# The weight lane of the feed-forward layers moves three steps at each turn in place of one

## The chip, the cores and the metric

The kernel runs on one core of a Trainium2 chip. The core has five instruction queues that work side by side: TensorE (PE, matrix products; PEld is its loading of weights), VectorE (DVE), ScalarE (ACT), GpSimd (POOL) and SyncE (SP, which here only issues DMA transfers). The metric is the device time of one execution in microseconds (us), the median over runs.

## The reference

One inference step of a two-layer decoder trunk, for a prompt of 1024 tokens with 16 meta tokens ahead of it, and for 8 running sequences with one new token each: 1048 columns in all, 1024 features. Layer 0 mixes with an SSD block (Mamba-2), layer 1 with a gated linear recurrence (RG-LRU). After each mixer stands the part that this case is about, a feed-forward layer of 4096 hidden features with a squared ReLU, between two RMS norms:

```python
def sq_relu_mlp(x, w1, w2):
    h = jax.nn.relu(x @ w1)
    return (h * h) @ w2

h = rms_norm(x, p["norm_ffn_pre"][i])
x = x + rms_norm(sq_relu_mlp(h, p["ffn_w1"][i], p["ffn_w2"][i]), p["norm_ffn_post"][i])
```

Everything is float32. The outputs are the new activations and the new states of both mixers.

## The kernel before

**Numbers in two halves.** A float32 operand is scaled by a power of two and split into two float16 tiles, a rounded half and the rest. A product then takes three float16 matmuls (half by half, half by rest, rest by half). The activations `U` (input of a feed-forward layer) and `H` (its hidden features) are kept like that, and so are the weights.

**Columns and strips.** The 1048 columns are worked in three pieces of 350, 350 and 348 (`c`). A weight matrix comes in strips of 256 output columns and 1024 input rows, 1 MB each. In a feed-forward layer the 4096 hidden features are worked in four blocks `b` of 1024. Each block takes four strips of `w1` (kind h in block 0, kind H after it), which produce `H`, and then four strips of `w2`, which add to the result `acc` (kind S in blocks 0 to 2, kind 2 in block 3).

**Units.** In blocks 1 to 3 the `w1` strips, and in blocks 0 to 2 the `w2` strips, go through `unit` (L1363): one strip with one column piece. It splits the product into two by two quadrants and works with seven smaller products in place of eight (Strassen's scheme; `product`, L380). It needs sums of weight quadrants (`wp`) beside the strip itself (`wh`), and sums of activations (`TT` from `U`, `HT` from `H`). The first product of a unit uses `wp`, the second `wh` with `TT` or `HT`. A unit of kind H has 84 matmuls, one of kind S about 90. It takes four of the eight PSUM banks (`mm`), so that two units can be on their way; ACT copies one product out (`z<-mm`), DVE adds the others into a tile `z`. For `w1`, ACT and DVE then form the squared ReLU and split it into `H`, and in the first two strips of a block `t_sums` (L1332) makes `HT`, its sums on POOL.

**The lane of the weights.** `wlane` (L406) is a Python generator that emits the instructions for one strip after the other. For each strip it emits, with a `yield` between the pieces:

1. the load of the 1 MB into one of two `ws` buffers (`load_strip`, L259; it is emitted while the strip ahead of it is converted);
2. the largest magnitude of each row, on DVE (`rm`, or `r` and `r4s` for kinds S and 2);
3. the scale (`strip_scale`, L264): a small matmul on PE spreads the rows' maxima (`mm<-ident,rm`), DVE takes the largest (`wgb`) and some ten tiny operations make the scale `s`, `sq`;
4. here the lane stops as long as more strips are ready than `ahead` allows. A strip with `wp` counts as two, and `ahead` is 3 within the blocks of units, 1 or 2 around them;
5. the sums (`sums`, L356): `wp` from ACT and DVE, three pairs of instructions, then four additions on POOL in place in `ws`;
6. the halves of the strip (`split`, L277): ACT writes the rounded half of `wh`, DVE the rest, in two instructions; for kinds S and 2 in four parts.

There are five `wh` buffers; a strip with `wp` takes two.

**Who moves the lane.** A main loop emits units and calls `tick` (L129) twice in each, once in its middle (in `unit`) and once at its end. `tick` moves each lane on by one `yield`: the lane of the weights, and others, such as the norm at a layer's border or the activation sums. A strip has three units and so six turns. When the main loop needs the next strip (`wneed`, L426) and it isn't ready, the lane is moved on until it is: whatever is left of a conversion is emitted there in one go. `first_phase` (L616) and `last_phase` (L567), at the start and the end of a layer, call `tick` as well.

**Order on the engines.** The order of emission is a priority. A planner in the framework lays the instructions of each engine out in time by its own cost estimates, and inserts all waits. On each engine it takes the instruction of highest priority among those whose inputs and buffers it expects to be there, so one of lower priority can move ahead into a gap. On the chip each engine then works through its list in order.

All instructions of this part are issued through one helper, so the profile has them all on L91 (earlier ones on L94): groups are told apart by tile names.

Of the kernel before, what the change touches and what calls it, by code (L numbers as in the profile page):

```python
# [60 lines left out]
class Carve:  # L61


    def __init__(self, tiles):
        self.free = [[t, 0] for t in tiles]
# [54 lines left out]
class Body:  # L120
    def __init__(self, ctx, tc, a):
        self.ctx, self.tc, self.nc, self.a = ctx, tc, Engines(tc), a
        self.lanes = []
        self.last_tab = None
        self.mmi = 0
        self.yfs = {}


    def tick(self):  # L129

        for lane in list(self.lanes):
            if next(lane, self) is self:
                self.lanes.remove(lane)

    def drain(self):
        while any(l is not self.wl for l in self.lanes):
# [1102 lines left out]
    def ffn(self, l):  # L1239
# [5 lines left out]
        HT = fp.tile([P, 3, NSUM, 3, 2, CW // 2], F16, name="HT")  # L1245
        U = self.U
        sctx = ExitStack()
        for b in range(4):
            H = fp.tile([P, 3, KT, 2, CW], F16, tag="H", name="H")
            rs = {}  # L1250

            def square(c, s, r):

                n = WC[c] // 2
                Hv = H[:, c, 2 * s:2 * s + 2, :, :2 * n].rearrange("p j s n -> p s j n")
                h = r.rearrange("p (j n) -> p j n", j=2)
                parts = [(0, n, 2 * n), (1, 0, 2 * n)] if self.summed(b, s) else [(slice(0, 2), 0, 2 * n)]
                nc.scalar.activation(Hv[:, 0], h, AF.Square)
                nc.scalar.activation(r, r, AF.Square)
                for j, o, e in parts:  # L1260
                    nc.vector.tensor_tensor(Hv[:, 1, j, o:e], h[:, j, o:e], Hv[:, 0, j, o:e], op=OP.subtract)
                if self.summed(b, s):
                    t = self.t_sums(r.rearrange("p (i n) -> p i n", i=4), Hv[:, :, 0, :n], HT[:, c, s, :, :, :n])
                    next(t)
                    self.lanes.append(t)

            def evac(s, w, m, c, ps):
                n = WC[c]
                if m == 0:
                    rs[s, c] = fp.tile([P, 2 * CW], F32, tag="r", name="r", bufs=RBUF)  # L1270
                r = rs[s, c]
                nc.scalar.activation(r[:, m * n:m * n + n], ps, AF.Relu, scale=w[2])
                if m:
                    square(c, s, rs.pop((s, c))[:, :2 * n])

            if b == 0:
                self.first_phase([self.wneed() for _ in range(3)], act, evac)
                sp = sctx.enter_context(tc.tile_pool(name=f"sum{l}", bufs=1, side="right", reuse_waits="tile"))
                TT = sp.tile([P, 3, 4, 3, 2, CW // 2], F16, name="TT")
                w = self.wneed()  # L1280
                for c in range(3):
                    for m in range(2):
                        ps = self.mm()
                        self.bundle(ps[:, :WC[c]], w[0], m, act, c)
                        evac(3, w, m, c, ps[:, :WC[c]])
                        self.tick()
                tl = self.input_sums(U, TT, fp)
                self.lanes.append(tl)
                self.ahead = 3
            else:  # L1290
                while tl in self.lanes:
                    self.tick()
                for s in range(4):
                    w, _, ti = self.wneed()
                    for c in range(3):
                        z = self.unit(w, self.parts(U, TT, c), c, 4, fp)
                        nc.scalar.activation(z, z, AF.Relu, scale=ti)
                        square(c, s, z)
                        self.tick()
            if b < 3:  # L1300
                for s in range(4):
                    w, inv, _ = self.wneed()
                    for c in range(3):
                        z = self.unit(w, self.parts(H, HT, c), c, NSUM, fp)
                        z = z.rearrange("p (m n) -> p m n", m=2)
                        o = acc[:, c, 2 * s:2 * s + 2, :WC[c]]
                        if b == 0:
                            nc.scalar.activation(o, z, AF.Copy, scale=inv)
                        else:
                            nc.vector.scalar_tensor_tensor(o, z, inv, o, op0=OP.mult, op1=OP.add)  # L1310
                        self.tick()
                if b == 2:
                    self.ahead = 2
            else:
                sctx.close()
                hact = self.act_of(H)
                self.open_bnd()

                def evac2(piece, mm, ps, inv, o):
                    c, lo, hi = piece  # L1320
                    nc.vector.scalar_tensor_tensor(o, ps, inv, acc[:, c, mm, lo:hi], op0=OP.mult, op1=OP.add)

                ws = [self.wneed()[:2] for _ in range(4)]
                if l == 0:
                    self.last_phase(ws, hact, 1, self.xd[0], self.xd[1], 2, evac2)
                else:
                    self.last_phase(ws, hact, 3, self.xd[2], [self.a["y01"][0], self.a["y01"][1], self.a["y2"]], None, evac2)
                    self.drain()
                    self.bndctx.close()
# [62 lines left out]


    def lru(self):
        nc, tc, ty = self.nc, self.tc, self.tiny
        a, v = self.a, self.v
        sctx = ExitStack()
# [154 lines left out]
        for s in range(4):  # L1552
            w, inv, _ = self.wneed()
# [118 lines left out]
```

## Time and profile before

| | |
|---|---|
| median of 3 runs | 2915.55 us (2909.4 to 2917.27) |
| the profiled execution | 2920.68 us |
| its span in the profile | 2918.8 us |
| mean granted TensorE clock | 0.954 |
| PE, DVE, ACT, POOL busy | 90%, 75%, 46%, 23% |
| DMA | 229 MB, 79 GB/s in the mean |

The span is the time from the first to the last instruction. "Granted clock" is the share of full speed that the chip gave TensorE. A table by stage cuts the span at given times and lists each engine's busy time within. A timeline row has the start, the length, the engine, the line, the operation with its output and inputs, and the count of instructions merged in it; brackets show how long the engine had been idle before, and what ended that. In a row of groups the busy time and the mean length of one in nanoseconds stand before the last bar, the idle time ahead of the group behind it.

### The profile page before, as it was taken

To read this page: it belongs to the slowest core of one execution; us is meant where nothing else is said; L and a number is where in the kernel's file an instruction comes from. 1 tells how busy PE (TensorE), PEld (TensorE's weight loads), DVE (VectorE), ACT (ScalarE), POOL (GpSimd) and SP (SyncE) were. 2 spreads that over 40 slices of the span, in tenths; PEclk is the share of its full clock that TensorE was granted. 3 is DMA by queue.
4 is the path that set the end of the run, shared out by engine and by line. 5 is a ranking of instruction groups with operands and counts; after the bars stand their busy time and mean duration, and the time that the engine had idled before them with its cause. 6 is when DMAs were issued, how large, how long until landed. Compare 5 with 4: busy or idle time off the path is not lost. (4 is left out here: it accounts for less than half of the span.)

```text
span 2918.8 us, 56796 instructions
## 1 busy us (share of the span) xinstructions
PE 2636.0 (90%) x23318; PEld 2089.8 (72%) x23318; DVE 2184.9 (75%) x5152; ACT 1329.8 (46%) x2148; POOL 668.5 (23%) x863
## 2 busy tenths in 40 slices
PE   5999999999999999889788899989999879889898
PEld 2666666666666668779788776665667879889776
DVE  6888977897745867778777689678785777777676
ACT  4544555545543453452442444577564343352342
POOL 3212212221110035421311100132024531221201
PEclk9999999999999999899898999999999989899899
DMA  3233233332345210111021133111220111111122
GB/s 139 77 105 109 86 100 110 108 108 94 113 159 222 100 58 30 45 44 45 30 88 59 45 107 112 65 42 56 94 101 16 45 44 45 45 32 57 36 80 92
DMA packets 52756, 229.14 MB, mean 79 GB/s; under 512 B 9056, under 2 KB 18416, under 8 KB 31632
## 3 DMA queue, kind: packets, MB, share of 16 engines
q1 hardware_dynamic: 46112, 190.81, 19.0%
q0 software_dynamic: 6384, 34.71, 3.0%
q8 instruction: 182, 2.98, 0.4%
q14 instruction: 78, 0.64, 0.1%
HBM read 186.28 MB, written 39.22 MB: 77 GB/s over the span
## 5 line engine op out<-in xcount | busy, mean ns | idle before, releaser
L91 PEld LDWEIGHTS <-wh 128*128 128x128 f16 x17040 | 1534.1, 100 | 639.5 <-ACT wh L91 104.5
L91 PE MATMUL mm<-U,wh 128*128 128x350 f16 (+3 forms) x7056 | 1015.2, 301 | 12.2 <-ACT rr L91 11.6
L91 PE MATMUL mm<-H,wh 128*128 128x175 f16 (+5 forms) x5664 | 569.4, 255 | 8.9 <-DVE wh L91 8.8
L91 POOL TENSOR_TENSOR ws<-ws 128x256 f32<-128x256 f32 (+1 forms) x192 | 214.1, 1115 | 656.5 <-DVE wp L91 602.9
L91 DVE TENSOR_TENSOR z<-z,mm 128x175 f32<-128x175 f32 (+3 forms) x648 | 232.8, 372 | 97.8 <-ACT z L91 71.2
L91 PEld LDWEIGHTS <-wp 128*128 128x128 f16 x3888 | 305.2, 98 | 0.5 <-DVE wp L91 0.2
L91 PE MATMUL mm<-TT,wh 128*128 128x175 f16 (+1 forms) x1728 | 191.0, 262 | 119.1 <-ACT wh L91 80.7
L91 DVE SCALAR_TENSOR_TENSOR wh<-ws,s,wh 128x256 f16<-128x256 f32 x256 | 141.5, 596 | 29.9 <-ACT wh L91 29.7
L91 ACT ACTIVATE z<-z,ti 128x700 f32<-128x700 f32 (+1 forms) x72 | 63.2, 877 | 188.4 <-DVE z L91 188.4
L91 PE MATMUL mm<-U,wp 128*128 128x175 f16 (+1 forms) x1728 | 146.8, 240 | 0.0
L91 PE MATMUL mm<-HT,wh 128*128 128x175 f16 (+1 forms) x864 | 102.8, 248 | 39.4 <-DVE wh L91 22.8
L91 DVE SCALAR_TENSOR_TENSOR wh<-ws,sw,wh 128x1024 f16<-128x1024 f32 x94 | 117.6, 1279 | 26.6 <-ACT wh L91 26.6
L91 DVE TENSOR_REDUCE rm<-ws 128x1 f32<-128x2048 f32 x40 | 91.3, 2283 | 51.6 <-DMA ws<-w 47.8
L91 ACT ACTIVATE z<-mm 128x175 f32<-128x175 f32 x144 | 43.7, 303 | 173.9 <-PE mm L91 173.9
L91 ACT ACTIVATE wh<-ws,s 128x512 f16<-128x512 f32 x128 | 85.5, 712 | 80.1 <-POOL ws L91 65.5
L91 ACT ACTIVATE pre<-mm,undo 128x8 f32<-128x8 f32 (+1 forms) x104 | 46.7, 476 | 155.2 <-PE mm L91 155.2
L91 DVE TENSOR_TENSOR H<-z,H 128x175 f16<-128x175 f32 (+5 forms) x120 | 90.8, 773 | 33.8 <-ACT z L91 18.1
L91 DVE SCALAR_TENSOR_TENSOR wh<-ws,sq,wh 128x1024 f16<-128x1024 f32 x48 | 61.5, 1282 | 63.4 <-ACT wh L91 63.4
L91 DVE SCALAR_TENSOR_TENSOR conv<-pre,ssmall,conv 128x1072 f32<-128x1072 f32 x78 | 105.9, 1358 | 0.0
L91 ACT ACTIVATE wh<-ws,sw 128x2048 f16<-128x2048 f32 x47 | 93.8, 1999 | 18.2 <-DVE sw L91 16.0
L91 DVE TENSOR_SCALAR L<-L,ncs 128x128 f32<-128x128 f32 (+1 forms) x288 | 93.5, 369 | 8.3 <-DMA L<-csd 8.3
L91 DVE TENSOR_TENSOR ss<-ss,sqt 128x350 f32<-128x350 f32 (+3 forms) x154 | 76.5, 504 | 29.5 <-ACT sqt L91 28.7
(284 smaller groups left out, 4181.0 us busy)
## 6 DMA issues: line engine op xcount, KB each, us to landing
ws<-w SPq DMA_DIRECT2D x64, 1024.0 KB, 4.9
ws<-w_ssd_in SPq DMA_DIRECT2D x24, 1024.0 KB, 6.8
L<-csd SPq DMA_DIRECT2D x64, 256.0 KB, 3.4
ws<-w_lru_in SPq DMA_DIRECT2D x12, 1024.0 KB, 4.8
xd<-xc POOLq DMA_DIRECT2D x6, 1400.0 KB, 5.0
xc<-xd SPq DMA_DIRECT2D x6, 1400.0 KB, 6.3
h<-ssd_h SPq DMA_DIRECT2D x8, 1024.0 KB, 4.9
bc<-bcd SPq DMA_DIRECT2D x8, 1024.0 KB, 5.2
```

Of the source, the lines that this page charges most:

```text
L91: r = f(*args, **kw)
```

## The change

`tick` moves the lane of the weights by `wsteps` yields in place of one; the other lanes still move by one. `wsteps` is 1 at the start, becomes 3 where a feed-forward layer begins and goes back to 1 where the recurrent mixer begins. Nothing else changes: the same instructions are emitted, in another order. In the feed-forward layers, a strip's instructions are emitted within the units of the strip ahead of it.

```diff
@@ -123,14 +123,17 @@
         self.lanes = []
         self.last_tab = None
         self.mmi = 0
+        self.wsteps = 1
         self.yfs = {}
 
 
     def tick(self):
 
         for lane in list(self.lanes):
-            if next(lane, self) is self:
-                self.lanes.remove(lane)
+            for _ in range(self.wsteps if lane is self.wl else 1):
+                if next(lane, self) is self:
+                    self.lanes.remove(lane)
+                    break
 
     def drain(self):
         while any(l is not self.wl for l in self.lanes):
@@ -1245,6 +1248,7 @@
         HT = fp.tile([P, 3, NSUM, 3, 2, CW // 2], F16, name="HT")
         U = self.U
         sctx = ExitStack()
+        self.wsteps = 3
         for b in range(4):
             H = fp.tile([P, 3, KT, 2, CW], F16, tag="H", name="H")
             rs = {}
@@ -1392,6 +1396,7 @@
 
 
     def lru(self):
+        self.wsteps = 1
         nc, tc, ty = self.nc, self.tc, self.tiny
         a, v = self.a, self.v
         sctx = ExitStack()
```

## The prediction

> **What bounds the kernel now.** I read the busy line of the page first, then the table by stage, cut at the twelve blocks of feed-forward strips that go through `unit` (layer 0: S of b 0, H and S of b 1, H and S of b 2, H of b 3; then the same six of layer 1; H is a block of four `w1` strips, S one of four `w2` strips).
>
> ```profile
> PE 2636.0 (90%) x23318; PEld 2089.8 (72%) x23318; DVE 2184.9 (75%) x5152; ACT 1329.8 (46%) x2148; POOL 668.5 (23%) x863
> ```
>
> ```profile
> 1105.00:1197.00 92.00, 82.84 (x1004) 79.80 (x1003) 68.63 (x173) 36.98 (x76) 54.15 (x76) 0.93 0.10 36
> 1197.00:1304.00 107.00, 84.90 (x1005) 82.18 (x1006) 77.04 (x181) 50.77 (x81) 36.16 (x43) 0.89 0.12 41
> 1304.00:1396.00 92.00, 86.10 (x1090) 83.90 (x1090) 72.18 (x182) 23.36 (x50) 15.75 (x16) 0.98 0.13 47
> 1396.00:1506.00 110.00, 88.44 (x1014) 85.24 (x1014) 81.87 (x185) 49.76 (x79) 31.49 (x38) 0.88 0.17 59
> 1506.00:1610.00 104.00, 92.41 (x1082) 90.04 (x1082) 76.95 (x186) 24.07 (x51) 18.19 (x19) 0.90 0.18 62
> 1610.00:1712.00 102.00, 85.91 (x1018) 82.21 (x1019) 69.42 (x166) 43.52 (x63) 16.83 (x12) 0.92 0.15 53
> 2219.00:2311.00 92.00, 82.49 (x1008) 79.94 (x1007) 68.65 (x174) 36.98 (x76) 54.54 (x76) 0.94 0.11 36
> 2311.00:2419.00 108.00, 87.23 (x1008) 84.70 (x1005) 76.79 (x180) 50.41 (x80) 36.29 (x43) 0.87 0.11 40
> 2419.00:2511.00 92.00, 84.57 (x1090) 82.30 (x1090) 72.22 (x182) 23.43 (x51) 15.74 (x16) 1.00 0.14 47
> 2511.00:2621.00 110.00, 89.57 (x1006) 86.57 (x1006) 78.49 (x180) 49.79 (x80) 33.89 (x40) 0.86 0.11 40
> 2621.00:2713.00 92.00, 84.66 (x1090) 82.30 (x1090) 72.27 (x182) 21.86 (x50) 15.46 (x16) 1.00 0.14 47
> 2713.00:2817.00 104.00, 88.44 (x1014) 84.95 (x1015) 70.75 (x167) 44.84 (x64) 16.60 (x13) 0.89 0.15 50
> sum 1205.00, PE 1037.57 PEld 1004.11 DVE 885.25 ACT 455.77 POOL 345.08; mean PE 86.46 PEld 83.68 DVE 73.77 ACT 37.98 POOL 28.76
> ```
>
> The columns are length, then busy time and count of PE, PEld, DVE, ACT, POOL, then granted clock. TensorE sets these stages, but in 1205 us it is idle for 1205.0 - 1037.6 = 167.4 us, and the H blocks are the long ones: 102 to 110 us at a clock of 0.86 to 0.92, against 92 us at 0.93 to 1.00 for five of the six S blocks. The waits of PE, first in layer 0 (1105 to 1712), then in layer 1 (2219 to 2817), say why:
>
> ```profile
> PE mm L91 <- ACT wh L91: 52.3, 18, 7.2
> PE mm L91 <- DVE wh L91: 33.7, 42, 1.9
> PE mm L91 <- ACT wh L91: 44.7, 17, 7.2
> PE mm L91 <- DVE wh L91: 36.2, 40, 1.9
> ```
>
> Together 166.9 us: all of the idle time is PE waiting for the f16 halves `wh` of the next strip. The timeline of one H strip shows what is late:
>
> ```profile
> 1429.93 0.33 SPq L261 DMA_DIRECT2D ws<-w  x1
> ...
> 1431.21 1.97 PE L91 MATMUL mm<-TT,wh 128*128 128x175 f16 x12
> ...
> 1436.11 0.22 PE L91 MATMUL mm<-ident,rm 128*128 128x128 bf16 x1
> ...
> 1436.75 2.27 DVE L91 TENSOR_REDUCE rm<-ws 128x1 f32<-128x2048 f32 x1
> ...
> 1437.09 1.08 PE L91 MATMUL mm<-TT,wh 128*128 128x175 f16 x12
> ...
> 1438.01 1.07 PE L91 MATMUL mm<-U,wh 128*128 128x175 f16 x12
> ...
> 1439.80 0.28 DVE L91 TENSOR_REDUCE wgb<-mm 128x1 f32<-128x128 f32 x1
> ...
> 1441.52 0.71 ACT L91 ACTIVATE wp<-ws,sq 128x512 f16<-128x512 f32 x1
> ...
> 1447.25 5.81 POOL L91 TENSOR_TENSOR ws<-ws 128x512 f32<-128x512 f32 x4 [0.68 <-ACT HT L91]
> ...
> 1453.10 2.00 ACT L91 ACTIVATE wh<-ws,sq 128x2048 f16<-128x2048 f32 x1 [3.38 <-POOL ws L91]
> ...
> 1455.16 0.47 PE L91 MATMUL mm<-TT,wh 128*128 128x175 f16 x2 [5.15 <-ACT wh L91]
> ...
> 1457.69 1.28 DVE L91 SCALAR_TENSOR_TENSOR wh<-ws,sq,wh 128x1024 f16<-128x1024 f32 x1
> ```
>
> Load and reduction are no problem. The load at 1429.93 serves the strip after next, and its reduction, at 1436.75, stands on DVE ahead of the scale (`wgb`, 1439.80) of the strip before it. So the planner lets an instruction run ahead of its turn where its engine has room. TensorE never has room: the small matmul that spreads a strip's maximum (`mm<-ident,rm`, 1436.11) runs at its turn, one unit after the strip's start. Behind it stand scale, `wp`, four POOL sums, the ACT half and two DVE halves: from 1436.11 to 1458.97, 22.9 us, of which 1441.52 to 1458.97, 17.5 us, are conversion proper. A strip's own matmuls take less: 12 of them 0.92 us (1437.09 to 1438.01), the 3 x 84 of an H strip 19.3 us. And after a wait PE is slow: 12 matmuls take 1.97 us at 1431.21 and 1.08 at 1437.09.
>
> **The change, part by part.** No instruction is added and none removed; the lane's steps move forward in the order of emission. An H strip has 12 lane steps, an S strip 10, and a strip of three units gives 6 turns: 6 steps until now, the rest in a burst in `wneed`, when PE already stands before the next strip. With 18 steps the conversion of strip n+1 is out by the fourth turn within strip n, the next reduction by the fourth and the next scale matmul by the fifth, all ahead of n's end. There the lane stops, since `ahead` is 3 and a pair costs 2. So the order on TensorE changes by one 0.22 us matmul a strip, moved forward by about one unit and a half; at the start of strip n its scale is known, and `wp` can start as soon as the two `wh` buffers of strip n-1 are free, at n's first matmul.
>
> *H strips.* Conversion proper from there takes, by the rows above, 13.6 us to the end of the ACT half (1441.52 to 1455.10) and 17.5 to the last DVE half, against 19.3 us of matmuls. The wait goes, with 1.9 us to spare at the last half and 5.7 at the first. *S strips*, from one of b 1:
>
> ```profile
> 1335.83 0.22 PE L91 MATMUL mm<-ident,rm 128*128 128x128 bf16 x1
> ...
> 1340.80 1.87 ACT L91 ACTIVATE wp<-ws,s 128x128 f16<-128x128 f32 x6 [5.37 <-DVE s L91]
> ...
> 1350.65 0.25 PE L91 MATMUL mm<-HT,wh 128*128 128x175 f16 x1 [1.91 <-DVE wh L91]
> ...
> 1350.75 0.49 DVE L91 SCALAR_TENSOR_TENSOR wh<-ws,s,wh 128x256 f16<-128x256 f32 x1
> ```
>
> Here conversion takes 1340.80 to 1351.24, 10.4 us of about 20.7 us of matmuls; the wait of 1.91 goes with room left.
>
> *Slow clock.* At 0.92 us for 12, a block's matmuls take 0.0767 us each: an H block (1008) 77.3 us, an S block (about 1084) 83.1, all twelve 963 us. PE is busy for 1037.6, so 75 us go to the lower clock. With 167 us of waits, that is 242 us, the most that can be won.
>
> *What takes its place.* DVE has 77 to 82 us of work in the H blocks of b 1 and 2, as much as PE will have. How full can the two run? The fullest stretch, ahead of the recurrent layer, from 1712 to 1800:
>
> ```profile
> 1712.00:1800.00 88.00, 85.11 (x554) 54.42 (x553) 78.12 (x163) 37.06 (x64) 1.23 (x3) 0.98 0.32 118
> ```
>
> PE is at 0.967 there, DVE at 0.888. So I take each block as the longer of PE/0.967 and DVE/0.888. H: 86.7, 92.2 and 79.9 (PE) in layer 0, 86.4, 88.3 and 79.9 in layer 1, together 513 us against 641 now. S: 85.9 (PE), five times. The S block at 1506 stays near 100 instead of 104: gate strips stand between its strips, both `ws` buffers are taken, and the next load starts only when a conversion ends. Together 529.5 against 564. That saves 128 + 34.5 = 162 us. I take off a remaining wait of 0.4 us for each of 48 strips, 19 us, between none and the one or two us that S strips show now. Net 143 us.
>
> *Other places that run at three steps.* First and last phases of the layers: the lane is held by `ahead` at 1 or 2, the same conversions come out a few turns sooner, and the 19 us of DVE between 1712 and 1800 that convert the last strips begin under the last H strip. I put that at zero, between a gain and a loss of 5 us.
>
> 2920.7 (profiled execution) - 143 = 2778. The median of the runs shown stands 5 us below that execution, which gives 2773; I put down 2775.
>
> **Rivals.** (1) *POOL holds ACT, and ACT holds DVE.* ACT waits in order for the POOL sums; from 1396 to 1506:
>
> ```profile
> L91 ACT ACTIVATE wh<-ws,sq 128x2048 f16<-128x2048 f32 x4 | 8.0, 2004 | 17.0 <-POOL ws L91 17.0
> ```
>
> That is 4.25 us a strip. Now it falls where PE waits anyway; moved into the strip, the copies `z<-mm` queue behind it, and DVE's additions behind those. Where DVE is the bound (four H blocks) this costs 17 us each, where PE is (two), about 7: 82 us of the 143, leaving 2855. Against it: POOL will start nearer to the strip's beginning, and S blocks have DVE time to spare.
>
> (2) *POOL lengthens DVE.* Two-input DVE operations grow beside POOL:
>
> ```profile
> L91 DVE TENSOR_TENSOR HT<-z,HT x24: 690/705/1805, 1215.1 to 2580.3; 128x525 f16<-128x525 f32 x16, 128x522 f16<-128x522 f32 x8
> ```
>
> The longest is 1.1 us over the median. If four such operations a strip now meet the four POOL sums, DVE has 4.4 us more in each H strip: again 17 to 18 us in four blocks, 70 in all, 2845. The Trainium skill (SBUF — State Buffer, "Who interferes with whom") has the mechanism: a DVE instruction with two SBUF inputs and a reading GpSimd instruction exclude each other for the whole instruction. By that rule, the trace agrees that HT can more than double; no row says that more of them will meet.
>
> (3) *No effect.* The planner already reorders, so the turn may not matter: 2915. Against it stands the scale matmul at 1436.11, exactly behind the first unit.
>
> (4) *Slower: results stay in PSUM.* Conversions come in lumps ahead of the additions that empty the banks. A strip's delay is then the ACT hold 4.25, `wp` 2.3, `wh` 2.6 and a reduction 2.3 us, 11.4 us, against 6.4 us until the next-but-one unit needs the banks. PE would stop for 5 us in each of 48 strips, S too: 240 us of idle time for the present 167, plus half as much clock loss again as now (37): 2915 + 110 = 3025. It decides from a delay of 6.4 + 3.5 = 9.9 us, 3.5 being 167 us over 48 strips. Against it: these pieces are spread over four turns and not one lump. A stop on the scale matmul would be its smaller relative, and the page-wide waits show little of it in all of the kernel:
>
> ```profile
> PE mm L91 <- DVE rm L91: 12.4, 5, 3.8
> ```
>
> **How the numbers follow.** Forecast 0.62, its own range 2715 to 2825; rival 1 0.15, rival 2 0.08, no effect 0.07, slower 0.08. The lower end is DVE at 0.95 (185 us saved), the gate block at 86 us too (14) and the gain of 5 in the phases; the floor is 2915 - 242 = 2673. The range reaches to 2870 and takes in rivals 1 and 2; it leaves out no effect and slower. Faster by over 0.3% (what a measurement of this kernel can tell from no change) holds the forecast and rivals 1 and 2: 0.85; same 0.07; slower 0.08.
>
> **What would show it.** Right: PE's waits for `wh` in the two layers fall from 167 to under 40 us, the clock of H blocks rises to 0.97 or more, H blocks of b 1 and 2 last 86 to 92 us with DVE near 0.89, and the scale matmul stands ahead of its strip's first unit. Rival 1: ACT still idle 3 to 4 us before `wh<-ws,sq` and DVE idle behind ACT `z`. Rival 2: the mean of HT and H rises. Rival 4: PE waits for DVE or ACT `z`, not for `wh`. The forecast is wrong if PE still waits for `wh` by more than 2 us a strip.

## The result, and the profile after

| | before | after |
|---|---|---|
| median of 4 runs | 2915.07 us (2909.4 to 2917.27) | 2873.96 us (2870.18 to 2878.27) |
| profiled execution | 2920.68 us | 2878.27 us |
| its span | 2918.8 us | 2876.5 us |
| mean granted TensorE clock | 0.954 | 0.964 |

The ratio is 0.9862, with a 95% interval from 0.9842 to 0.9882: 41 us faster. Faster was forecast, but by 140 us. The time lies 4 us outside the range, and less than a third of the gain came.

Where did it come from? These are the tables by stage of both kernels, cut now at the first matmul of a block that reads `HT` or `TT`. The two rows of each are the six blocks of layer 0 and of layer 1; the columns are those of the prediction. (The prediction's own first cut of each layer lay some 80 matmuls too late: 1205 us where these two rows hold 1212.) Before:

```profile
1098.10:1708.50 610.40, 524.00 (x6271) 507.60 (x6269) 447.63 (x1068) 230.35 (x402) 176.10 (x206) 0.91 0.14 48
2212.50:2814.10 601.60, 520.56 (x6272) 504.96 (x6270) 440.95 (x1064) 229.49 (x402) 175.58 (x206) 0.92 0.12 42
```

After:

```profile
1095.20:1675.50 580.30, 504.73 (x6272) 498.19 (x6270) 435.22 (x1054) 221.92 (x391) 175.59 (x210) 0.94 0.15 52
2184.10:2765.60 581.50, 506.55 (x6272) 498.75 (x6271) 428.15 (x1050) 221.42 (x390) 175.50 (x210) 0.95 0.13 44
```

The blocks fell from 1212.0 to 1161.8 us, by 50.2. The busy time of PE fell by 33.3 (1044.6 to 1011.3) at the same count of matmuls: the granted clock rose from 0.91 and 0.92 to 0.94 and 0.95. Its idle time fell by only 16.9 (167.4 to 150.5). The rest of the span grew by 7.9 us (2918.8 - 1212.0 = 1706.8; 2876.5 - 1161.8 = 1714.7).

So nearly all of the idle time is still there. The waits of PE over the whole kernel after the change (total, times, longest) give it another name:

```profile
PE mm L91 <- DVE z L91: 130.2, 61, 8.1
PE mm L91 <- DVE rm L91: 35.1, 11, 7.0
...
PE mm L91 <- DVE wh L91: 4.5, 6, 1.0
```

The same view before, page-wide:

```profile
PE mm L91 <- ACT wh L91: 97.2, 36, 7.2
PE mm L91 <- DVE wh L91: 69.9, 82, 1.9
...
PE mm L91 <- DVE rm L91: 12.4, 5, 3.8
```

The 167 us of waits for `wh` are gone, as forecast. In their place PE waits 130 us for `z` and 23 us more for `rm`. `z` is where DVE adds up what lies in the PSUM banks, so this is a wait for a bank to be emptied. The groups of instructions after the change say which instruction stands there, and who else stands:

```profile
L91 DVE SCALAR_TENSOR_TENSOR wh<-ws,sq,wh 128x1024 f16<-128x1024 f32 x48 | 61.5, 1281 | 111.8 <-ACT wh L91 111.8
L91 ACT ACTIVATE wh<-ws,sq 128x2048 f16<-128x2048 f32 x24 | 48.0, 2002 | 108.3 <-POOL ws L91 108.3
L91 PE MATMUL mm<-ident,rm 128*128 128x128 bf16 x99 | 22.4, 228 | 107.6 <-DVE z L91 71.4 <-DVE rm L91 35.1 <-ACT wh L91 1.0
```

The same three before:

```profile
L91 DVE SCALAR_TENSOR_TENSOR wh<-ws,sq,wh 128x1024 f16<-128x1024 f32 x48 | 61.5, 1282 | 63.4 <-ACT wh L91 63.4
L91 ACT ACTIVATE wh<-ws,sq 128x2048 f16<-128x2048 f32 x24 | 48.1, 2003 | 97.0 <-POOL ws L91 97.0
L91 PE MATMUL mm<-ident,rm 128*128 128x128 bf16 x99 | 21.8, 221 | 12.7 <-DVE rm L91 12.4 <-ACT wh L91 0.2
```

DVE waits longer for ACT, ACT longer for POOL, and PE, which stood 12.7 us at the small scale matmul, now stands 107.6 us there. One strip of the longest block shows the chain. The timeline after, from the middle of a strip of kind H:

```profile
1414.57 2.00 PE L91 MATMUL mm<-U,wp 128*128 128x175 f16 x24
...
1424.64 5.62 POOL L91 TENSOR_TENSOR ws<-ws 128x512 f32<-128x512 f32 x4 [0.68 <-ACT HT L91]
...
1424.75 1.07 PE L91 MATMUL mm<-TT,wh 128*128 128x174 f16 x12
...
1427.18 0.88 ACT L91 ACTIVATE z<-z,ti 128x700 f32<-128x700 f32 x1 [2.54 <-DVE z L91]
1430.30 2.00 ACT L91 ACTIVATE wh<-ws,sq 128x2048 f16<-128x2048 f32 x1 [2.25 <-POOL ws L91]
...
1432.34 1.28 DVE L91 SCALAR_TENSOR_TENSOR wh<-ws,sq,wh 128x1024 f16<-128x1024 f32 x1 [5.19 <-ACT wh L91]
1432.89 0.29 ACT L91 ACTIVATE z<-mm 128x175 f32<-128x175 f32 x1
...
1433.54 0.33 DVE L91 TENSOR_TENSOR z<-z,mm 128x175 f32<-128x175 f32 x1
...
1433.92 0.27 PE L91 MATMUL mm<-ident,rm 128*128 128x128 bf16 x1 [8.11 <-DVE z L91]
```

Read it from the end. PE stops at 1425.8, behind the fourth product of the unit of column piece 2, and goes on at 1433.92 with the scale matmul of a later strip. That matmul asks for a PSUM bank. The next in turn is the first bank of the unit before (piece 1). The product that the copy is to fetch from there, the second half of the row at 1414.57, was ready at 1416.6. ACT copies it out at 1432.89, 16 us later. Ahead of that copy in ACT's list stand the ReLU of piece 0 (`z<-z,ti`), which had to wait for DVE's additions, and then the split of `wh`. At the split ACT waits 2.25 us for POOL, whose four additions run from 1424.64 to 1430.26, and its half takes 2.00 us: 4.25 us of the delay in this strip are the split. DVE's half of the split stands ahead of the addition that frees the bank, and DVE waits 5.19 us for ACT. PE works in order too: the scale matmul, whose result no strip needs yet, holds up the matmuls behind it.

The table by stage for layer 0 after the change (blocks S, H, S, H, S, H):

```profile
1095.00:1186.00 91.00, 84.48 (x1090) 84.06 (x1089) 71.81 (x164) 36.19 (x72) 62.48 (x86) 0.98 0.14 48
1186.00:1290.00 104.00, 85.09 (x1010) 83.41 (x1009) 72.49 (x185) 49.56 (x80) 32.69 (x40) 0.91 0.10 36
1290.00:1385.00 95.00, 86.74 (x1097) 85.27 (x1095) 76.44 (x186) 24.76 (x53) 15.40 (x16) 0.97 0.15 53
1385.00:1496.00 111.00, 85.09 (x1009) 83.66 (x1007) 81.46 (x197) 50.85 (x84) 33.27 (x40) 0.88 0.19 68
1496.00:1582.00 86.00, 83.07 (x1091) 82.50 (x1089) 71.84 (x168) 20.97 (x44) 15.55 (x16) 1.00 0.18 63
1582.00:1677.00 95.00, 81.64 (x1005) 80.53 (x1003) 62.52 (x164) 41.10 (x60) 16.41 (x12) 0.95 0.13 46
```

No engine is full in an H block: DVE is busy 72.5 of 104, 81.5 of 111 and 62.5 of 95 us, a share of 0.66 to 0.73. Only the S block at 1496 has PE close to its end.

### The profile page after: what moved, and what is told of

The parts are those of the page before. It is cut to its first block, busy times and chain, and to the rows that moved or that the text cites. A ratio compares the mean times of both kernels' runs of the same rounds, so it can differ in the third digit from the quotient of the medians.

```text
span 2876.5 us, 56770 instructions
## 1 busy us (share of the span) xinstructions
PE 2601.7 (90%) x23318; PEld 2073.5 (72%) x23318; DVE 2173.1 (76%) x5152; ACT 1322.5 (46%) x2148; POOL 662.3 (23%) x863
## 4 chain that ended last, share of the span: by engine, by line
DVE 33%; PE 30%; ACT 11%; POOL 10%; DMA 8%; issue 8%; SPq 0%; POOLq 0%; DVEq 0%; ACTq 0%
PE mm L91 25%; POOL ws L91 7%; DMA ws<-w 6%; DVE z L91 5%; DVE wh L91 4%; ACT wh L91 3%; PE yo L91 2%; DVE conv L91 2%; DVE wp L91 2%; ACT z L91 2%; DVE U L91 2%; DVE L L91 2%; DVE rm L91 2%; DVE xr L91 2%; POOL z L91 1%
## 5 line engine op out<-in xcount | busy, mean ns | idle before, releaser
L91 PEld LDWEIGHTS <-wh 128*128 128x128 f16 x17040 | 1499.8, 99 | 536.0 <-issue 105.2
L91 PE MATMUL mm<-U,wh 128*128 128x350 f16 (+3 forms) x7056 | 998.0, 298 | 18.7 <-ACT rr L91 11.7
L91 PE MATMUL mm<-H,wh 128*128 128x175 f16 (+5 forms) x5664 | 560.8, 254 | 11.5 <-DVE z L91 11.5
L91 PEld LDWEIGHTS <-wp 128*128 128x128 f16 x3888 | 322.3, 101 | 47.0 <-issue 23.3
L91 DVE TENSOR_TENSOR z<-z,mm 128x175 f32<-128x175 f32 (+3 forms) x648 | 227.2, 371 | 49.1 <-ACT z L91 42.6
L91 PE MATMUL mm<-U,wp 128*128 128x175 f16 (+1 forms) x1728 | 154.1, 247 | 25.3 <-DVE z L91 25.2
L91 DVE SCALAR_TENSOR_TENSOR wh<-ws,s,wh 128x256 f16<-128x256 f32 x256 | 148.8, 628 | 23.5 <-ACT wh L91 23.4
L91 PE MATMUL mm<-TT,wh 128*128 128x175 f16 (+1 forms) x1728 | 160.8, 242 | 5.3 <-DVE wh L91 4.5
L91 DVE SCALAR_TENSOR_TENSOR wh<-ws,sq,wh 128x1024 f16<-128x1024 f32 x48 | 61.5, 1281 | 111.8 <-ACT wh L91 111.8
L91 PE MATMUL mm<-ident,rm 128*128 128x128 bf16 x99 | 22.4, 228 | 107.6 <-DVE z L91 71.4
L91 PE MATMUL mm<-H,wp 128*128 128x175 f16 (+1 forms) x864 | 90.5, 241 | 16.3 <-DVE z L91 16.3
L91 ACT ACTIVATE wh<-ws,sw 128x2048 f16<-128x2048 f32 x47 | 93.7, 1998 | 16.9 <-DVE sw L91 14.7
L91 ACT ACTIVATE wh<-ws,sq 128x2048 f16<-128x2048 f32 x24 | 48.0, 2002 | 108.3 <-POOL ws L91 108.3
```

The source lines that it names most:

```text
L91: r = f(*args, **kw)
```

## The experiments

Two theories stood at the start. **Theory 1, the hold:** ACT's list and DVE's list hold the split of a strip ahead of the copies and additions that empty the banks, and the split waits for POOL. **Theory 2, the bank:** it is enough that the scale matmul asks for a bank in the middle of a strip. The expectations name a third, that DVE has no more room. The medians, and the ratio to the kernel before on the same chip:

| run | edit | us | ratio (95%) |
|---|---|---|---|
| e1_order | after + split behind the units' work, ACT and DVE | 2771.52 | 0.9538 (0.9519 to 0.9557) |
| e2_scale_by_dma | after, scale without PE and PSUM | 3023.33 | 1.0401 (1.0382 to 1.0421) |
| e3_no_pool_sums | after without the four additions | 2732.5 | 0.9391 (0.9366 to 0.9416) |
| e4_two_steps | two steps a turn | 2878.09 | 0.9902 (0.9883 to 0.9922) |
| e5_order_act | e1 on ACT alone | 2784.61 | 0.9553 (0.9537 to 0.9569) |
| e6_order_dve | e1 on DVE alone | 2815.89 | 0.9665 (0.965 to 0.9679) |
| e7_before_order | e1's rule, one step a turn | 2885.95 | 0.9903 (0.9884 to 0.9922) |
| e8_order_early | e1 with a looser rule | 2752.39 | 0.9443 (0.9429 to 0.9458) |
| e9_sums_on_dve | after, additions on DVE | 2780.88 | 0.9552 (0.9532 to 0.9572) |
| e10_early_dvesum | e8 and e9 | 2727.9 | 0.936 (0.9346 to 0.9374) |
| e11_before_dvesum | before, additions on DVE | 2790.5 | 0.9578 (0.9562 to 0.9594) |
| e12_one_step | e10 with one step a turn | 2766.16 | 0.9505 (0.9486 to 0.9523) |

The chips differ a little: the kernel before took 2908.4 us on the chip of e1 to e4, and 2912.8 to 2915.1 on the others. So differences from the changed kernel (0.9862) are taken below from the ratios, times 2915 us, and are good to a few us.

**e1_order.** `issue_after` puts an instruction behind a given one in its engine's list. Here the split goes behind the last ACT and the last DVE instruction of the units emitted so far. The scale matmul stays where it is.

```diff
+    def behind(self, last):
+        return nullcontext() if last is None else self.tc.issue_after(last.ins)
...
     def split(self, w, st, s, parts):
...
-            nc.scalar.activation(w[:, 0, sl], st[:, sl], AF.Copy, scale=s[:, i:i + 1])
+            with self.behind(self.lact):
+                nc.scalar.activation(w[:, 0, sl], st[:, sl], AF.Copy, scale=s[:, i:i + 1])
...
-                nc.vector.scalar_tensor_tensor(w[:, 1, o:o + h], ...
+                with self.behind(self.ldve):
+                    nc.vector.scalar_tensor_tensor(w[:, 1, o:o + h], ...
...
     def unit(self, w, BT, c, npair, fp):
...
-                nc.scalar.activation(p1, pa[:, 0], AF.Copy)
-                nc.vector.tensor_tensor(u2, p1, pa[:, 1], op=OP.add)
+                self.lact = nc.scalar.activation(p1, pa[:, 0], AF.Copy)
+                self.ldve = nc.vector.tensor_tensor(u2, p1, pa[:, 1], op=OP.add)
...
-        nc.vector.tensor_tensor(p1, p1, pd[:, 0], op=OP.add)
+        self.ldve = nc.vector.tensor_tensor(p1, p1, pd[:, 0], op=OP.add)
```

The last square (ACT) and the last part of the split into `H` (DVE) are taken down in the same way.

> The changed kernel with one thing added: the ACT half of a strip's split may not stand on ACT's list ahead of the ACT work of the last unit emitted before it, nor the DVE half ahead of that unit's DVE work. Nothing is computed differently. Theory 1 (hold): the split stands too early in the lists of ACT and DVE, waits there for the POOL sums, and the copies and additions that empty PSUM wait behind it; then DVE's idle time ahead of the H strips' wh (111.8 us) falls under 40 us, PE's waits for DVE z and rm (165 us) fall under 80, and the time to 2780 to 2820. Theory 2 (bank): PE stops because the scale's small matmul asks for a ninth PSUM bank within a unit; that stays, so 2865 to 2885. Theory 3 (DVE has no more room): 2865 to 2885 as well.

It took 2771.52 us, by the ratios 94 less than the changed kernel, and a little under the range of theory 1. The three groups of e1:

```profile
L91 DVE SCALAR_TENSOR_TENSOR wh<-ws,sq,wh 128x1024 f16<-128x1024 f32 x48 | 62.2, 1330 | 2.4 <-ACT wh L91 1.0
L91 ACT ACTIVATE wh<-ws,sq 128x2048 f16<-128x2048 f32 x24 | 47.8, 1992 | 0.7 <-POOL ws L91 0.7
L91 PE MATMUL mm<-ident,rm 128*128 128x128 bf16 x99 | 22.0, 224 | 37.9 <-DVE rm L91 26.5 <-DVE z L91 10.4 <-ACT wh L91 0.4
```

The waits in front of the split went from 111.8 to 2.4 and from 108.3 to 0.7 us, and with them the scale matmul's wait for `z` from 71.4 to 10.4, though it still asks for the same banks. Theory 1 holds, and theory 2 falls as a cause by itself: asking for the bank costs little where the bank is emptied in time. One thing more changed: DVE's halves of the S strips take 516 ns in e1 and 628 in the changed kernel, and DVE's busy time fell by 30 us (2173.1 to 2143.2). A part of the gain may come from that, and e1 doesn't separate it.

**e2_scale_by_dma.** The scale is spread over the partitions by two small transfers through DRAM, for kinds H and S, so that it needs neither PE nor a bank.

```diff
-        ps = self.mm()
-        nc.tensor.matmul(ps[:, :P], gmax...to_broadcast([P, P]), ...)
-        nc.vector.tensor_reduce(gb, ps[:, :P], axis=AX.X, op=OP.max)
...
+        nc.sync.dma_start(d.rearrange("o p -> p o"), gmax)
...
+        nc.sync.dma_start(rb, d.to_broadcast([P, P]))
+        nc.vector.tensor_reduce(gb, rb, axis=AX.X, op=OP.max)
```

> The changed kernel, but for kinds H and S the row maxima are spread over the partitions by two small DMA transfers through DRAM in place of the matmul on PE, so no PSUM bank is asked for. Theory 2 (bank): the 107.6 us that PE stands ahead of that matmul go, 2770 to 2800. Theory 1 (hold): PE runs on until the next unit asks for the same bank, at most three products or 2.7 us later, in some 40 strips where it stops; the copies are as late as before: 2830 to 2870.

It missed both expectations: 3023.33 us. What the scale's reduction on DVE waited for in e2, and how long a transfer took from issue to landing:

```profile
  DMA rb<-rd: 373.7, 48
...
DMA to landing us min/median/max: 4.0/4.5/5.7
```

DVE stood 7.8 us in the mean for each of the 48 strips at a reduction whose transfers weren't in yet, with the units' additions behind it in its list. So the run doesn't settle the bank; e1 does. But it is the same fault at another place: an instruction put into an in-order list ahead of work that was ready.

**e3_no_pool_sums.** The four additions in `ws` are left out (this part of the weights' sums isn't computed).

```diff
-            tt(o, a, b, op=op)
```

> The changed kernel without the four POOL additions that make the sums of weight quadrants in place (this part of the computation is left out; all else runs as before). Theory 1 (hold): nothing holds the split any more, 2760 to 2800, and ACT's idle time ahead of wh behind POOL goes. Theory 2 (bank): the scale's matmul still asks for its bank within the unit, PE's waits ahead of it stay over 70 us, 2850 to 2880. Theory 3 (DVE has no more room): DVE's work is the same but for the lengthening beside POOL, some 10 to 20 us: 2850 to 2870.

2732.5 us, 137 less than the changed kernel and under all three ranges. It is more than e1 brought; here the weights are also in time: PE waits 0.4 us for `wh`, where e1 left 47.4. PE still waits 33.4 us for `z` and 31.3 for `rm`. The six S blocks take 82.7 to 84.4 us; the prediction had 83.1 us as the time of their matmuls at full clock.

**e4_two_steps.**

```diff
-        self.wsteps = 3
+        self.wsteps = 2
```

> The changed kernel with two steps a turn in place of three: the twelve steps of an H strip then fill its six turns, and the split comes out at the last. Theory 1 (hold): the split stands later in the lists, so DVE's idle time ahead of wh falls by a third to a half, and little of the wait for wh comes back: 2830 to 2860. Theory 2 (bank): the scale's matmul moves to the first turn, within a unit as well: 2865 to 2885. If only being early matters, it is between one step (2915) and three (2874): 2890.

All expectations were missed: 2878.09 us, no better than three steps. The split's groups in e4:

```profile
L91 DVE SCALAR_TENSOR_TENSOR wh<-ws,sq,wh 128x1024 f16<-128x1024 f32 x48 | 61.6, 1295 | 103.0 <-ACT wh L91 103.0
L91 ACT ACTIVATE wh<-ws,sq 128x2048 f16<-128x2048 f32 x24 | 48.0, 2002 | 124.4 <-POOL ws L91 124.4
```

The hold is no shorter (124.4 us on ACT), and PE's waits are mixed: 68.5 us for `z`, 81.8 for `wh`. Emitting the split at a later turn did not bring ACT to it behind the POOL sums. That fits a planner that puts it where it expects its inputs by its own estimates; what those estimates are, no run shows.

**e5_order_act and e6_order_dve** use the rule of e1 on one engine each.

In e5 the DVE half of the split is free, in e6 the ACT half:

```diff
-                with self.behind(self.ldve):
+                with self.behind(None):
```

```diff
-            with self.behind(self.lact):
+            with self.behind(None):
```

> As the run with the split held behind the last unit's work (2771.5 us), but on ACT's list alone; DVE's half of the split stands where the planner puts it. If the hold starts on ACT, which waits for POOL and keeps the copies behind it, and DVE only follows (its half needs ACT's half, and the planner knows that), nearly all of the gain stays: 2770 to 2795. If DVE's own list is the place of the hold, at most half of it: 2810 to 2850.

> As that run, but on DVE's list alone; ACT's half of the split stays ahead of the copies. If the hold starts on ACT: the copies are still 4.5 us late in each H strip, DVE waits for them (ACT z) in place of wh, 2830 to 2870. If DVE's own list is the place: 2770 to 2800.

The rule on ACT alone gives 90 us (2784.61) where e1 gave 94; the intervals of the two ratios overlap. That is what was expected of a hold that starts on ACT. ACT then waits 0.7 us for POOL, as in e1, and DVE 4.6 us ahead of its halves: with ACT in time there is little left to order on DVE. The rule on DVE alone gives 57 us (2815.89), between its two expectations. The split on ACT in e6, and then the waits of DVE and PE there:

```profile
L91 ACT ACTIVATE wh<-ws,sq 128x2048 f16<-128x2048 f32 x24 | 48.0, 2000 | 113.0 <-POOL ws L91 113.0
DVE z L91 <- ACT z L91: 103.3, 40, 5.6
PE mm L91 <- DVE wh L91: 75.5, 34, 7.3
...
PE mm L91 <- DVE z L91: 20.6, 13, 5.2
```

The hold on ACT is unbroken and the copies are late: DVE waits 103.3 us for them, against 42.6 in the changed kernel. Yet PE's waits for `z` fall from 130.2 to 20.6 us. So a late copy alone stops PE little; it did so where DVE's additions stood behind the split as well. In place of those stops PE waits 75.5 us for halves of `wh` that come late. The two lists are links of one chain, from POOL to ACT to DVE, and breaking either link takes most of the stops on the banks away. That fits 90 and 57 making more than 94.

**e7_before_order.** The kernel before, one step a turn, with the rule of e1 (edit as in e1).

> The kernel before (one step a turn) with the same rule of order on ACT and DVE. Its splits are emitted behind all units of the strip, so the rule puts them behind the last unit's work; PE waits for wh as before or longer: 2905 to 2940. If the order alone were what counts, without the early start, it would come near 2800.

Missed: 2885.95 us, 28 less than before where little or nothing was expected. The hold was in the kernel before already, and the rule takes it off: the wait of ACT for POOL falls from 97.0 to 15.4 us:

```profile
L91 ACT ACTIVATE wh<-ws,sq 128x2048 f16<-128x2048 f32 x24 | 47.8, 1990 | 15.4 <-POOL ws L91 15.4
```

Alone, the rule brings 28 us and the three steps 41; together they bring 135 (e1). Each hides what the other would give: without the steps the conversion still comes too late (PE waits 114.4 us for `wh` in e7), without the rule it comes early and stands in the way.

**e8_order_early.** The rule looks only at a unit's copy out of PSUM (ACT) and its last addition (DVE), no longer at the squares and the split into `H`.

```diff
-                self.lact = nc.scalar.activation(r, r, AF.Square)
+                nc.scalar.activation(r, r, AF.Square)
...
-                    self.ldve = nc.vector.tensor_tensor(Hv
+                    nc.vector.tensor_tensor(Hv
```

> The changed kernel with the split held behind the last unit's copy out of PSUM and its last addition only, not behind its squares. In the run with the full rule PE still waits 47 us for wh, because the split now comes late in some H strips. If those waits can be had without the hold: 2735 to 2765. If an earlier split holds the next copies again: 2775 to 2820.

2752.39 us, as expected if the waits for `wh` can be had without the hold. In this kernel only the instructions that empty the banks need to go first; PE's waits for `wh` are 37.4 us, against 47.4 with the full rule.

**e9_sums_on_dve.** The changed kernel, its lists unruled, with the additions on DVE.

```diff
-        tt = nc.gpsimd.tensor_tensor
+        tt = nc.vector.tensor_tensor
```

> The changed kernel with the four additions of weight quadrants on DVE in place of POOL; all is computed. The split then follows DVE's own work and no longer waits for a slow engine, while DVE gets 4 x 0.5 us more in each H strip and 4 x 0.3 in each S strip, about 80 us in all, less what two-input DVE operations lose beside POOL. If the hold by POOL is the cause: 2790 to 2830, between the run without these sums (2732) and the changed kernel. If DVE's room is the bound: 2880 to 2950.

2780.88 us, 90 less than the changed kernel and better than expected. The groups by form, after:

```profile
L91 DVE SCALAR_TENSOR_TENSOR wh<-ws,s,wh 128x256 f16<-128x256 f32 x256 | 148.8, 628 | 23.5 <-ACT wh L91 23.4
L91 POOL TENSOR_TENSOR ws<-ws 128x512 f32<-128x512 f32 x96 | 132.1, 1376 | 278.3 <-DVE wp L91 262.7 <-issue 7.3 <-ACT HT L91 2.7
L91 POOL TENSOR_TENSOR ws<-ws 128x256 f32<-128x256 f32 x96 | 78.2, 814 | 343.8 <-DVE wp L91 330.7 <-DVE r4s L91 7.4
```

In e9:

```profile
L91 DVE SCALAR_TENSOR_TENSOR wh<-ws,s,wh 128x256 f16<-128x256 f32 x256 | 117.5, 502 | 11.1 <-ACT wh L91 11.1
L91 DVE TENSOR_TENSOR ws<-ws 128x512 f32<-128x512 f32 x96 | 66.6, 694 | 0.6
L91 DVE TENSOR_TENSOR ws<-ws 128x256 f32<-128x256 f32 x96 | 40.5, 422 | 0.5
```

An addition takes half as long on DVE (1376 to 694 ns, 814 to 422). The Trainium skill (GPSIMD Engine Reference, "3.1 Elementwise — side-by-side cycle accounting") gives 1.96 for that ratio at 2048 f32 elements; these rows agree with 1.98 and 1.93. DVE takes on 107.1 us, and 31 of them come back in its halves of `wh`, which are shorter without these additions on POOL (628 to 502 ns). The Trainium skill (SBUF — State Buffer, "Who interferes with whom") says that DVE instructions with two SBUF inputs and GpSimd instructions that read SBUF exclude each other; this agrees with it, though no run tests the meeting alone. In all, DVE's busy time rose by 42 us (2173.1 to 2215.4), and the kernel became 90 us faster: DVE had time, the chain had none. That rules out the third theory.

**e10_early_dvesum.** e8 and e9 together.

> The best kernel so far (split behind the last unit's copy and last addition, 2752.4 us) with the four additions on DVE as well. If POOL's length still costs there (27 us of ACT's idle time and 34 us of PE's waits for wh): 2725 to 2750. If DVE is full by now, in the H blocks of b 1 and 2 above all: 2755 to 2800.

2727.9 us, ratio 0.936, in the first of the two ranges: the best of all, 146 us faster than the changed kernel, and no slower than e3, which has none of these additions at all. The table by stage of e10, the two rows of blocks:

```profile
1096.70:1610.90 514.20, 488.27 (x6273) 485.23 (x6272) 456.44 (x1152) 225.79 (x397) 73.24 (x114) 0.98 0.17 59
2115.30:2620.00 504.70, 486.88 (x6292) 483.98 (x6289) 448.42 (x1151) 226.77 (x400) 73.30 (x114) 0.98 0.15 52
```

The clock is 0.98, PE idles 43.8 us of 1018.9, and DVE is at 0.888 (904.9 / 1018.9), the share that the prediction took as its bound. What is left of PE's waits in e10:

```profile
PE mm L91 <- DVE rm L91: 35.7, 13, 6.0
...
PE mm L91 <- DVE wh L91: 17.0, 13, 3.2
```

The wait for `rm` is the price of a scale matmul that now stands ahead of its strip's reduction.

**e11_before_dvesum and e12_one_step.** With POOL out of the chain, what are the three steps worth? e11 is the kernel before with the edit of e9, e12 is e10 with `wsteps` at 1.

> The kernel before (one step a turn) with the four additions on DVE in place of POOL, to see what three steps are worth where POOL holds nothing (with three steps: 2780.9 us). Conversion proper gets shorter by some 3.5 us in an H strip (5.8 us of POOL become 2 of DVE), so PE's waits for wh, 167 us, fall by about 80 with the clock loss behind them: 2820 to 2860. If the prediction's gain for the steps (143 us) holds where nothing else stands in the way, the difference to 2780.9 is what the remaining waits are, 40 to 80 us; if the steps are worth no more than the 41 us measured, 2815 to 2825.

> The best kernel (three steps, split held behind the last unit's copy and addition, sums on DVE; 2727.9 us) with one step a turn again: what the steps alone are worth where neither POOL nor the order holds anything. The kernel before with the sums on DVE took 2790.5. If the steps are worth by themselves what takes the waits for wh away: 2775 to 2795, 50 us or more over 2727.9. If the order alone does it: 2730 to 2750.

e11 missed its expectation: at one step a turn, moving the additions brings 123 us by itself (ratio 0.9578), and beside it e9's three steps are worth some 10 us, with intervals of the ratios that overlap. With the order set as well, one step gives 2766.16 (between the two expectations) and three steps 2727.9: there the change is worth some 40 us. Waits of PE in e12:

```profile
PE mm L91 <- ACT wh L91: 47.8, 17, 5.4
PE mm L91 <- DVE wh L91: 21.2, 43, 1.3
```

These 69 us of waits for late weights are what the steps take away (17.0 and 5.0 remain in e10), less what they add in waits for `rm`.

## Why the prediction was wrong, step by step

**What bounds the kernel: right.** PE waited for `wh`, and those waits went from 167 to 6 us. The forecast had allowed 40.

**Order and conversion time: right.** The scale matmul stands within the strip ahead, and the conversion is over before the strip needs it. Rival 3, no effect, is out.

**What takes its place: this step failed.** It took each block as the longer of PE/0.967 and DVE/0.888, with a remaining wait of 0.4 us a strip. That asks how full an engine can be. It doesn't ask whether, in each list, ready work stands behind work that isn't. The H blocks were put at 513 us in all and took 607.3; DVE is at 0.69 of them, far from 0.888. The S blocks, with gates, were put at 529.5 and took 554.5. Remove the hold, and they come near: 549.1 and 528.4 in e1, 499.1 for S in e10. That e1's time lies so near the forecast is partly chance: its H blocks are 36 us longer than forecast, and 15 us were won outside the blocks against the kernel before, which no run explains.

**Rival 1 had the cause.** ACT stands idle ahead of the split as it said (4.5 us for each of 24 strips, against the 4.25 in the prediction). The path behind that is in part another. It had DVE stand idle behind the late copies (ACT `z`). That wait, before and after the change:

```profile
DVE z L91 <- ACT z L91: 71.2, 57, 5.6
DVE z L91 <- ACT z L91: 42.6, 38, 2.0
```

It fell, and what grew is DVE's wait ahead of its own half of the split (63.4 to 111.8 us). Two more things were wrong in its price of 82 us and its chance. It counted the delay for H strips alone, as time of the engine that was the bound there, and left out where such a delay ends: in a PSUM bank that isn't emptied, which stops PE whoever is the bound. That is the place of rival 4, whose "smaller relative", a stop on the scale matmul, became the main wait (12.7 to 107.6 us). And the argument against it, that POOL would start nearer to the strip's beginning, is not enough: in the strip shown above the split's place in ACT's list lies ahead of a copy whose product had long been ready. Measured by e1, the hold costs some 94 us, of which a part may be shorter DVE instructions.

**Rival 4** has its sign: PE waits for DVE `z` and no longer for `wh`. Its size didn't come. It put 5 us of stops on each strip, 240 us in all, and a loss from 3.5 us a strip (a delay of 9.9 us, 6.4 of them free). The stops for `z` and `rm` make 165 us, 3.4 a strip, in place of the 167 for `wh` before, so there was no loss.

**Rival 2** isn't the cause. The lengthening exists (628 against 502 ns in e9), but DVE's busy time fell with the change (2184.9 to 2173.1 us) where rival 2 needs 70 us more. The lengthening was there before the change too (596 ns).

**The clock** of the H blocks was to rise to 0.97 or more. It came to 0.88 to 0.95 in them. In layer 0 it was lowest in the block in which PE stood longest (0.88 with 25.9 us of idle time in 111) and 1.00 in the one in which it stood least (2.9 us in 86), and it came to 0.98 in e10. Why it rose by 0.03 with the change, though PE's waits by the rows above are nearly as long in sum (169.8 us in 78 stops, 179.5 in 123 before), no run shows.

**Smaller terms:** the S block with gates between its strips was put near 100 us and took 86; the phases outside the blocks were put at zero, within 5 us, and lost 7.9; the distance from the profiled execution to the median was put at 5 us and is 4.3.

**Still open:** why the planner puts the split ahead of the copies. That its estimates have POOL too fast or PE too slow is argued from e4, not shown.

## What to carry to other kernels

Emitting work earlier makes it early only where its inputs are early; until then it stands in an in-order list, and everything behind it waits. Before moving a chain forward, look in each engine's list at what will stand behind its slowest link, above all at the instructions that empty PSUM, and either order those first or take the slow engine out of the chain. A bound from busy shares says how fast a stage could be, not that it will get there.

## What the hardware showed that I had not expected

- The four additions on POOL, 5.5 us in an H strip and 3.3 in an S strip on an engine that is busy for 23% of the span: moving them to DVE took 123 us off the kernel before (e11) and 90 us off the changed one (e9).
- Two dependent transfers of 512 bytes and 64 KB through DRAM (the second landed 4.5 us after issue in the median) made DVE stand 7.8 us in the mean in each of 48 strips (e2), far more than the 0.22 us matmul that they replaced.
